# Two recurrence projections taken from the mixer's first block and turned by transposes

## The chip, the cores and the metric

The kernel runs on one core of a Trainium2 chip. The metric is the time of one execution in device microseconds (us). Before the change the median of three runs is 940.21 us (939.73 to 942.36).

## The reference, cut to what matters

The model is an encoder of two layers over 256 tokens of width 1024. Each layer is a half-weighted SwiGLU block, a mixer and a second half-weighted SwiGLU block, each with its own norm; here is the mixer.

```
h = rms_norm(x, mix_norm[l])
proj = h @ w_in[l]                       # 256 x 1792
xr, gate, q, k, v = split(proj, 512 | 512 | 512 | 128 | 128)
y_rec = recurrent_group(xr, gate, ...)   # conv of 4 taps along time, gates, scan in both directions
y_att = windowed_gqa(q, k, v, ...)       # 8 heads, 2 of keys and values
x = x + concat(rms_norm(y_rec), rms_norm(y_att)) @ w_out[l]
```

The change concerns the first 256 of the 512 columns of xr, that is two of its four tiles of 128 channels, and k and v together (256 columns).

## The kernel before, in words

All matrix products are made to near float32 precision from two parts: a value is split into a rounded high part (fp32r) and the rest, and three products are added: high by high, low by high, high by low. So each product of 8 tiles of 128 rows takes 24 matmuls. The engines are named as in the profile: PE is TensorE, DVE is VectorE, ACT is ScalarE, POOL is GpSimd, SP is SyncE.

Weights come in as 1 MB pieces called raw (256 columns of w_in for 1024 rows) by DMAs that SP issues (L248) into three buffers. ACT writes the high part wh (L303; for a few, DVE does, L301) and DVE the low part wl (L304); this happens some units ahead of use (prefetch, prep_one). A raw buffer is loaded anew when the last half made from it is done. Halves lie in a ring of eight slots; the first two halves of the mixer, named kv, lie in two other tiles (EXTRA).

At a boundary between stages (L588 to L620) TensorE finishes the last stage's output, then transposes the normed activations of tokens 0 to 127 (L535), runs head(0), transposes those of tokens 128 to 255, and runs head(1). In the mixer, head(t) (L846) makes keys and values with the tokens as rows: 24 matmuls, each with 256 columns of weights moving (L552). Both token halves lie in one PSUM bank, that ACT copies to kv_t at once (L855). In a SwiGLU stage head(t) (L690) has 24 matmuls of 512 columns (L697), and a bank for each token half.

Then the mixer's body follows the list ORDER (L59), unit by unit. A letter and a digit are one unit: x is one tile of xr, computed with channels as rows (unit, L840: 24 matmuls of 256 columns, L560 to L562, into a bank of its own), after which DVE runs the convolution on it straight out of PSUM in four steps (conv: L877, L879 twice, L880). k turns the keys by two transposes (L864). q is one tile of queries, l the gate matmuls of the recurrence (L900 to L902), L one pair of heads' logits (L965 to L967) with the softmax's first steps on DVE (L974), g the gate, P and V the rest of the attention. Units take their banks in turn from four (bank("gc"): two of ps_g, two of ps_c).

The order on PE, SP and POOL is the order in which the code is written. On ACT and DVE a scheduler sets it when the program is built; on the chip it is fixed, and each engine takes its instructions strictly in that order.

Of the kernel before, what the change touches and what calls it, by code (L numbers as in the profile page):

```python
# [8 lines left out]
F32 = mybir.dt.float32  # L9
F32R = mybir.dt.float32r  # L10
AF = mybir.ActivationFunctionType
# [6 lines left out]
KD = DM // 128  # L18
DFF = 2816
NM = DFF // 128  # L20
T = 256
# [34 lines left out]
CUT = 3  # L56
RCUT = 1
EARLY = 1
ORDER = "x0 k0 x1 q0 l0 q1 l1 L0 x2 L1 x3 g0 l2 P0 q2 l3 V0 P1 s0 L2 g1 c0 c1 q3 V1 P2 L3 c2 y0 g2 y1 V2 P3 g3 c3 V3 D0 y2 y3 r0 O0 r1 O1 r2 r3 R0 R1 R2 R3 S0".split()  # L59
HEAD = 2  # L60
VO = 6
VG = 1
# [5 lines left out]
def encoder_kernel(  # L68
# [31 lines left out]
    pe, act, dve, pool = nc.tensor, nc.scalar, nc.vector, nc.gpsimd  # L100

    def P(name, bufs, **kw):
        return ctx.enter_context(tc.tile_pool(name=name, bufs=bufs, **kw))
# [9 lines left out]
    sum_p = P("sum", 1)  # L113
# [11 lines left out]
    def bank(pool_):  # L125
        if pool_ == "gc":
            turn.append(turn.pop(0))
            pool_ = turn[0]
        return {"a": ps_a, "b": ps_b, "g": ps_g, "c": ps_c}[pool_].tile([128, 512], F32, tag=pool_, name="ps_" + pool_)
# [9 lines left out]
    def add_raw(src, shape):  # L139
        raws.append((src, shape))  # L140
        return len(raws) - 1

    def add_half(name, pieces, form):
        index[name] = len(halves)
        halves.append((name, pieces, form))
        if name[0][1] != 1 or name[1:] not in EXTRA:
            ring.append(name)
            turns[name] = len(ring) - 1

    def cols(w, c):  # L150
        return add_raw(w[:, c:c + 256].rearrange("(k p) c -> p k c", p=128), "kc")

    def rows(w, r):
        return add_raw(w[r:r + 256, :].rearrange("(k p) c -> p k c", p=128), "rc")

    def col_half(name, r, j):
        add_half(name, [(r, j * 128, 0, 128)], "kc")

    def head_half(name, r, j):
        add_half(name, [(r, j)], "kh")  # L160
# [26 lines left out]
        down(NM // 2 - 1)  # L187

    def plan_mix(st, wi, wo):
        r = cols(wi, 1536)  # L190
        for j in range(2):
            head_half((st, "kv", j), r, j)
        chunk = {}

        def chunk_of(n, p):
            if (n, p) not in chunk:
                chunk[n, p] = cols(wi, {"x": 0, "g": 512, "q": 1024}[n] + p * 256)
            return chunk[n, p]

        for n, i in ORDER:  # L200
            i = int(i)
            if n in "xg":
                col_half((st, {"x": "xr", "g": "gt"}[n], i), chunk_of(n, i // 2), i % 2)
            elif n == "q":
                add_half((st, "q", i), [(chunk_of("q", h), i * 64, h * 64, 64) for h in range(2)], "kc")
        for p in range(4):
            r = rows(wo, p * 256)
            for j in range(2):
                add_half((st, "o", 2 * p + j), [(r, j)], "rc")
# [103 lines left out]
    def prefetch(target):  # L313
        while state["half"] <= min(target, state["cap"], len(halves) - 1):
            j = state["half"]
            n = turns.get(halves[j][0], 0)
            if n >= SLOTS and ring[n - SLOTS] not in used:
                return
            with ExitStack() as behind:
                for ins in state["behind"]:  # L320
                    behind.enter_context(tc.issue_after(ins.ins))
                prep_one()

    def W(*name):
        prefetch(index[name] + state["ahead"])
        return slot_t[name]

    def done(name):
        used.add(name)
        del slot_t[name]  # L330

    eye_t = const.tile([128, 128], F32, name="eye_t")
# [159 lines left out]
    cur = {}  # L492
# [52 lines left out]
    def natural(outs, ws, t):  # L545
        ts_ = slice(t * 128, (t + 1) * 128)
        xh, xl = cur["h"], cur["l"]
        for p in range(3):
            for k in range(KD):
                for dst, w in zip(outs, ws):  # L550
                    c = slice((k % 4) * 256, (k % 4) * 256 + 256)
                    pe.matmul(dst, (xh, xh, xl)[p][:, k, ts_], w[k // 4][p % 2][:, c],  # L552
                              start=(p == 0 and k == 0), stop=(p == 2 and k == KD - 1))

    def proj(dst, w, t0, t1):
        wh, wl = w
        xh, xl = cur["h"], cur["l"]
        for k in range(KD):
            ks = slice(k * 128, (k + 1) * 128)
            pe.matmul(dst, wh[:, ks], xh[:, k, t0:t1], start=(k == 0), stop=False)  # L560
            pe.matmul(dst, wh[:, ks], xl[:, k, t0:t1], start=False, stop=False)  # L561
            pe.matmul(dst, wl[:, ks], xh[:, k, t0:t1], start=False, stop=(k == KD - 1))  # L562
# [264 lines left out]

    def mix(l):
        st = (l, 1)
        ps_x = {}  # L830
        xch_t, xcl_t = {}, {}
        xc_t, ge_t, a_t, yh_t, yl_t = {}, {}, {}, {}, {}
        q_t = mix_p.tile([128, NT, T], F32R, tag="q", name="q_t")
# [3 lines left out]
        kv_t = mix_p.tile([128, 2, 256], F32, tag="kv", name="kv_t")  # L837
        late = {}

        def unit(name, i):  # L840
            ps = bank("gc")[:, 0:T]
            proj(ps, W(st, name, i), 0, T)
            done((st, name, i))
            return ps

        def head(t):  # L846
            if t == 0:
                ps_x["kv"] = bank("gc")
            ps = ps_x["kv"]
            natural([ps[:, t * 256:t * 256 + 256]], [[W(st, "kv", j) for j in range(2)]], t)  # L850
            if t == 1:
                for j in range(2):
                    done((st, "kv", j))
                new_tiles()
                act.activation(out=kv_t.rearrange("p t c -> p (t c)"), in_=ps, func=AF.Copy)  # L855

        def new_tiles():
            late["w"] = w_p.tile([128, 2 * NT, T], F32, tag="w", name="w_t")
            late["i"] = mix_p.tile([128, 2 * NT, T], F32, tag="i", name="i_t")
# [6 lines left out]
            dve.tensor_sub(out=kl_t, in0=ps[:, 0:T], in1=k_t.bitcast(F32))  # L866

        def xr(i):
            ps = unit("xr", i)
            with tc.high_priority(offset=MIXF):  # L870
                conv(i, ps)

# [202 lines left out]
        def att_mm(k, t, hfs, fin):  # L1075
            if t not in acc_a:
                acc_a[t] = [bank("ab"[t]) for _ in range(2)]
            stream(acc_a[t], yh_t[4 + k], yl_t[4 + k], W(st, "o", 4 + k), t, hfs, k == 0, k == 3)
            if fin:
                done((st, "o", 4 + k))  # L1080

        def tail(t, part):
            if part in (0, 1):
                for k in range(4):
                    att_mm(k, t, (0,), False)
            if part == 0 and "O1" not in ORDER:
                o_split(1)
# [10 lines left out]
        def body():  # L1098
# [17 lines left out]
            def stats(_):  # L1116
# [5 lines left out]
                    "L": att_logits, "P": att_pt, "V": att_pv, "D": den, "O": o_split, "f": lambda _: turn.reverse()}  # L1122
            for n, i in ORDER:
                step[n](int(i))
                if n == "D":
                    load_gain(3 * l + 2)

        return head, body, tail, evac

    engines = mybir.EngineType  # L1130
    with tc.manual_schedule(engines={engines.PE, engines.SP, engines.Pool}):
# [18 lines left out]
        for s in range(3 * DEPTH):  # L1150
            _, body, tail, evac = stages[s]
            body()
            n = s + 1
# [53 lines left out]
```

## Time and profile before

| | |
|---|---|
| median of 3 runs | 940.21 us |
| profiled execution | 940.3 us |
| its span, first to last instruction | 938.5 us |
| granted TensorE clock, mean | 0.999 of full speed |
| PE busy | 925.9 us, 99% of the span |
| DVE busy | 696.5 us, 74% |
| ACT busy | 544.7 us, 58% |

A row of the timeline has the start of an instruction (or of several alike), its duration, the engine, the line of the kernel, the operation, the tile written and the tiles read, the shape and the count; in square brackets is the engine's idle time before it, and what ended that. Matmuls overlap, so the distance between the starts of two groups tells what a group costs, not its duration. The first layer's mixer runs from about 199.7 to 288 us; the second layer's has the same rows 458.8 us later.

### The profile page before, as it was taken

The numbers are of one execution on the slowest core, as the hardware profiler recorded it, in microseconds if no ns is written. First come the engines' busy times: TensorE is split into PE (matmuls) and PEld (weight loads), VectorE is DVE, ScalarE is ACT, GpSimd is POOL, SyncE is SP. The second block draws the span as 40 slices with busy tenths as digits, with TensorE's granted clock in tenths as the row PEclk, the third lists the DMA queues.
The fourth block names the chain that finished last, engine by engine and source line by source line (L and its number), as shares of the span: only waits on it lengthen the run. The fifth ranks groups of instructions, "written<-read, shape, count | busy, mean of one in ns | idle before, by whom it ended". The sixth has DMA issues, their size and how long they took to land.

```text
span 938.5 us, 13682 instructions
## 1 busy us (share of the span) xinstructions
PE 925.9 (99%) x5288; PEld 804.8 (86%) x5288; DVE 696.5 (74%) x1212; ACT 544.7 (58%) x1006; POOL 37.0 (4%) x58
## 2 busy tenths in 40 slices
PE   8999999999999999999999999999999999999997
PEld 7888888889988888888888888888999888888885
DVE  6877666759998866666688666666799887666663
ACT  7755555547865655555466555554687565555542
POOL 4100000000010000000030000000000100000000
PEclk9999999999999999999999999999999999999999
DMA  8966955614255866565557565655162566665521
GB/s 279 304 211 200 326 192 183 228 64 154 91 157 179 262 197 191 179 192 196 175 174 252 181 186 198 199 179 179 49 223 68 180 233 203 197 196 182 184 86 45
DMA packets 124993, 172.54 MB, mean 184 GB/s; under 512 B 3920, under 2 KB 108792, under 8 KB 124928
## 3 DMA queue, kind: packets, MB, share of 16 engines
q1 hardware_dynamic: 122192, 166.21, 54.7%
q0 software_dynamic: 2288, 4.87, 1.6%
q8 instruction: 41, 0.67, 0.3%
q10 hardware_dynamic: 448, 0.59, 0.2%
q14 instruction: 24, 0.20, 0.1%
HBM read 170.59 MB, written 3.16 MB: 185 GB/s over the span
## 4 chain that ended last, share of the span: by engine, by line
PE 92%; ACT 2%; DVE 2%; DMA 1%; issue 1%; POOL 0%; POOLq 0%; DVEq 0%; ACTq 0%
PE ps_g L572 16%; PE ps_c L572 15%; PE ps_g L571 7%; PE ps_c L571 7%; PE ps_a L581 5%; PE ps_a L583 4%; PE ps_a L582 4%; PE ps_b L582 4%; PE ps_b L583 4%; PE ps_b L581 4%; PE ps_g L697 2%; PE ps_c L697 2%; PE ps_a L1010 1%; PE ps_g L561 1%; PE ps_g L560 1%; PE ps_g L562 1%
## 5 line engine op out<-in xcount | busy, mean ns | idle before, releaser
L304 DVE TENSOR_TENSOR wl<-raw,wh 128x1024 fp32r<-128x1024 f32 (+1 forms) x320 | 367.4, 1157 | 106.3 <-ACT wh L303 101.9
L303 ACT ACTIVATE wh<-raw 128x1024 fp32r<-128x1024 f32 (+1 forms) x306 | 301.6, 1000 | 89.0 <-PE ps_b L583 61.8
L572 PE MATMUL ps_g<-xhl,wh 128*128 128x512 f32 x640 | 231.5, 396 | 1.5 <-DVE hl L746 1.5
L572 PE MATMUL ps_c<-xhl,wh 128*128 128x512 f32 x640 | 231.2, 396 | 0.0
L571 PE MATMUL ps_g<-xhl,wl 128*128 128x256 f32 x560 | 156.5, 279 | 0.0
L571 PE MATMUL ps_c<-xhl,wl 128*128 128x256 f32 x560 | 156.2, 279 | 0.0
L572 PEld LDWEIGHTS ps_g<-xhl,wh 128*128 128x128 f32 x640 | 120.3, 188 | 24.6 <-issue 1.7
L572 PEld LDWEIGHTS ps_c<-xhl,wh 128*128 128x128 f32 x640 | 120.2, 188 | 22.8
L571 PEld LDWEIGHTS ps_g<-xhl,wl 128*128 128x128 f32 x560 | 105.6, 189 | 3.5
L571 PEld LDWEIGHTS ps_c<-xhl,wl 128*128 128x128 f32 x560 | 105.5, 188 | 3.5
L581 PE MATMUL ps_a<-wh,hh 128*128 128x512 f32 x168 | 65.8, 392 | 0.0
L581 PE MATMUL ps_b<-wh,hh 128*128 128x512 f32 x168 | 65.7, 391 | 0.0
L583 PE MATMUL ps_b<-wh,hl 128*128 128x512 f32 x168 | 65.4, 389 | 0.0
L582 PE MATMUL ps_b<-wl,hh 128*128 128x512 f32 x168 | 65.4, 389 | 0.0
L583 PE MATMUL ps_a<-wh,hl 128*128 128x512 f32 x168 | 65.4, 389 | 0.0
L582 PE MATMUL ps_a<-wl,hh 128*128 128x512 f32 x168 | 65.4, 389 | 0.0
L757 ACT ACTIVATE sg<-ps_g 128x256 f32<-128x256 f32 x40 | 15.4, 385 | 63.5 <-PE ps_g L572 63.5
L757 ACT ACTIVATE sg<-ps_c 128x256 f32<-128x256 f32 x40 | 15.3, 383 | 55.3 <-PE ps_c L572 54.6
L758 DVE TENSOR_TENSOR sg<-ps_g,sg 128x256 f32<-128x256 f32 x40 | 17.0, 425 | 32.1 <-ACT sg L757 32.1
L757 ACT ACTIVATE su<-ps_c 128x256 f32<-128x256 f32 x40 | 15.3, 382 | 38.7 <-PE ps_c L572 38.7
L582 PEld LDWEIGHTS ps_a<-wl,hh 128*128 128x128 f32 x168 | 31.6, 188 | 6.9
L583 PEld LDWEIGHTS ps_a<-wh,hl 128*128 128x128 f32 x168 | 31.5, 188 | 6.9
(320 smaller groups left out, 1579.2 us busy)
## 6 DMA issues: line engine op xcount, KB each, us to landing
raw<-in_ffn_w_down_dram SPq DMA_DIRECT2D x44, 1024.0 KB, 5.0
raw<-in_ffn_w_gate_dram SPq DMA_DIRECT2D x43, 1024.0 KB, 5.4
raw<-in_ffn_w_up_dram SPq DMA_DIRECT2D x43, 1024.0 KB, 5.4
raw<-in_w_in_dram SPq DMA_DIRECT2D x14, 1024.0 KB, 5.4
raw<-in_w_out_dram SPq DMA_DIRECT2D x8, 1024.0 KB, 7.3
lb<-ld POOLq DMA_DIRECT2D x1, 2048.0 KB, 14.8
bias_t<-lb POOLq DMA_DIRECT2D x1, 1536.0 KB, 12.5
gain<-in_ffn_norm_dram SPq DMA_DIRECT2D x3, 512.0 KB, 4.3
```

What stands on the lines that cost most here:

```text
L303: act.activation(out=h3, in_=src, func=AF.Copy)
L304: dve.tensor_sub(out=l3, in0=src, in1=h3.bitcast(F32))
L560: pe.matmul(dst, wh[:, ks], xh[:, k, t0:t1], start=(k == 0), stop=False)
L561: pe.matmul(dst, wh[:, ks], xl[:, k, t0:t1], start=False, stop=False)
L571: pe.matmul(dst[:, 0:T], wl[:, ks], x2[:, 0, k, :], start=False, stop=False)
L572: pe.matmul(dst, wh[:, ks], x2[:, :, k, :], start=(k == 0), stop=(k == KD - 1))
L581: pe.matmul(acc[hf], ah[:, ts_], wh[:, cs], start=first, stop=False)
L582: pe.matmul(acc[hf], ah[:, ts_], wl[:, cs], start=False, stop=False)
L583: pe.matmul(acc[hf], al[:, ts_], wh[:, cs], start=False, stop=last)
L697: pe.matmul(ps, x, w[k // 2][p % 2][:, k % 2 * 512:k % 2 * 512 + 512], start=(p == 0 and k == 0), stop=(p == 2 and k == KD - 1))
L757: act.activation(out=s, in_=ps[:, T:2 * T], func=AF.Copy)
L758: dve.tensor_tensor(out=s, in0=ps[:, 0:T], in1=s, op=ALU.add)
```

## The change

Keys and values and the first two tiles of xr are computed together. The head of the mixer now has the form of a SwiGLU head: 24 matmuls per token half, with 512 columns of weights moving (256 of keys and values, 256 of xr), one bank per token half. Four weight halves are made for it (form "gu", each from both raw pieces, 256 columns of each) in place of two of keys and values and two of xr. ACT copies the two parts of each bank apart, to kv_t and to a new tile xn_x. The units x0 and x1 no longer multiply: each turns its tile by two transposes of 128 x 128. x0 and x1 write into the two halves of one bank, where x0 had a bank of its own and x1 another. ORDER puts q0 ahead of x0, and x2 ahead of the first gate unit l0; from x3 on it is the same.

```diff
-ORDER = "x0 k0 x1 q0 l0 q1 l1 L0 x2 L1 x3 g0 l2 P0 q2 l3 V0 ...
+ORDER = "q0 x0 k0 x1 q1 x2 l0 L0 l1 L1 x3 g0 l2 P0 q2 l3 V0 ...
...
     def plan_mix(st, wi, wo):
-        r = cols(wi, 1536)
-        for j in range(2):
-            head_half((st, "kv", j), r, j)
-        chunk = {}
+        chunk = {("x", 0): None}
+        r = cols(wi, 1536), cols(wi, 0)
+        for q in range(4):
+            add_half((st, "kv", q), [(r[0], q, 0), (r[1], q, 1)], "gu")
...
         for n, i in ORDER:
             i = int(i)
+            if n == "x" and i < 2:
+                continue
...
         def head(t):
-            if t == 0:
-                ps_x["kv"] = bank("gc")
-            ps = ps_x["kv"]
-            natural([ps[:, t * 256:t * 256 + 256]], [[W(st, "kv", j) for j in range(2)]], t)
+            ps = bank("gc")
+            ts_ = slice(t * 128, (t + 1) * 128)
+            w = [W(st, "kv", q) for q in range(4)]
+            for p in range(3):
+                for k in range(KD):
+                    x = cur["l" if p == 2 else "h"][:, k, ts_]
+                    pe.matmul(ps, x, w[k // 2][p % 2][:, k % 2 * 512:k % 2 * 512 + 512],
+                              start=(p == 0 and k == 0), stop=(p == 2 and k == KD - 1))
+            act.activation(out=kv_t[:, t, :], in_=ps[:, 0:T], func=AF.Copy)
+            xn_x[t] = sum_p.tile([128, T], F32, tag=("sg", "su")[t], name="xn_x")
+            act.activation(out=xn_x[t], in_=ps[:, T:2 * T], func=AF.Copy)
             if t == 1:
-                for j in range(2):
-                    done((st, "kv", j))
+                for q in range(4):
+                    done((st, "kv", q))
                 new_tiles()
-                act.activation(out=kv_t.rearrange("p t c -> p (t c)"), in_=ps, func=AF.Copy)
...
         def xr(i):
-            ps = unit("xr", i)
+            if i < 2:
+                if i == 0:
+                    ps_x["x"] = bank("gc")
+                ps = ps_x["x"][:, i * T:(i + 1) * T]
+                for t in range(2):
+                    pe.transpose(ps[:, t * 128:(t + 1) * 128], xn_x[t][:, i * 128:(i + 1) * 128], eye_t)
+            else:
+                ps = unit("xr", i)
             with tc.high_priority(offset=MIXF):
                 conv(i, ps)
```

Line numbers in the following lists are those of the file they belong to: the changed one has conv at L892 to L895, k0's transposes at L872 and those of x0 and x1 at L882. A name's number tells buffers apart, and "waits" names the engine whose count an instruction waits for.

On PE before the change, from the end of x0 over the keys' transposes into x1:

```order
L562 MATMUL ps_g<-xhl,wl 128x256
L864 MATMUL ps_c<-eye_t,kv_t 128x128 x2
L560 MATMUL ps_g<-xhl,wh 128x256
L561 MATMUL ps_g<-xhl,wh 128x256
L562 MATMUL ps_g<-xhl,wl 128x256
```

And on PE after it, from the end of q0 over x0, k0 and x1 to the start of q1:

```order
L564 MATMUL ps_c_2200<-xhl_2080,wl_2010 128x256
L882 MATMUL ps_g_2227<-eye_t_111,xn_x_2144 128x128 [waits PE_49]
L882 MATMUL ps_g_2227<-eye_t_111,xn_x_2196 128x128 [waits Activation_49]
L872 MATMUL ps_c_2239<-eye_t_111,kv_t_1973 128x128 [waits PE_49]
L872 MATMUL ps_c_2239<-eye_t_111,kv_t_1973 128x128
L882 MATMUL ps_g_2227<-eye_t_111,xn_x_2144 128x128 [waits DVE_49]
L882 MATMUL ps_g_2227<-eye_t_111,xn_x_2196 128x128
L562 MATMUL ps_g_2255<-xhl_2080,wh_2015 128x256 [waits PE_49]
```

Where x1 multiplied without a wait, it now has two transposes into the bank of x0 (ps_g_2227), the first of which waits for DVE. The count in the program is the one that the last of x0's four conv steps (L895) gives.

On DVE before the change, from x0's conv to the start of x1's:

```order
L877 TENSOR_SCALAR xc_2211<-ps_g_2186,par_117 128x256 [waits PE_49]
L866 TENSOR_TENSOR kl_t_1972<-ps_c_2220,k_t_1971 128x256 [waits Activation_49]
L879 SCALAR_TENSOR_TENSOR xc_2211<-ps_g_2186,par_117,xc_2211 128x254 [waits DVE_49]
L879 SCALAR_TENSOR_TENSOR xc_2211<-ps_g_2186,par_117,xc_2211 128x255 [waits DVE_49]
L880 SCALAR_TENSOR_TENSOR xc_2211<-ps_g_2186,par_117,xc_2211 128x255 [waits DVE_49]
L301 CAST wh_2312<-raw_2157 128x1024 [waits DMAHW3_49]
L877 TENSOR_SCALAR xc_2250<-ps_g_2225,par_117 128x256 [waits PE_49]
```

And on DVE after it, from the low part of the weights of x3 over x0's conv to the start of x1's:

```order
L306 TENSOR_TENSOR wl_2165<-raw_2007,wh_2164 128x1024 [waits Activation_49]
L303 CAST wh_2256<-raw_2168 128x1024 [waits DMAHW3_49]
L892 TENSOR_SCALAR xc_2230<-ps_g_2227,par_117 128x256 [waits PE_49]
L1120 SCALAR_TENSOR_TENSOR ql_t_1970<-ps_c_2200,q_t_1969 128x256 [waits Activation_49]
L894 SCALAR_TENSOR_TENSOR xc_2230<-ps_g_2227,par_117,xc_2230 128x254 [waits DVE_49]
L874 TENSOR_TENSOR kl_t_1972<-ps_c_2239,k_t_1971 128x256 [waits Activation_49]
L894 SCALAR_TENSOR_TENSOR xc_2230<-ps_g_2227,par_117,xc_2230 128x255 [waits DVE_49]
L306 TENSOR_TENSOR wl_2257<-raw_2168,wh_2256 128x1024
L895 SCALAR_TENSOR_TENSOR xc_2230<-ps_g_2227,par_117,xc_2230 128x255 [waits DVE_49]
L306 TENSOR_TENSOR wl_2288<-raw_1981,wh_2287 128x8x64
L904 TENSOR_TENSOR xcl_2236<-xc_2230,xch_2235 128x256 [waits Activation_49]
L892 TENSOR_SCALAR xc_2246<-ps_g_2227,par_117 128x256 [waits PE_49]
```

The queries' low part (L1120), the keys' (L874) and a weight split of 128 x 1024 (L306) now stand between the four steps of x0's conv, and the cast of a raw piece that is still on its way (L303) ahead of them.

## Rows read from the trace of the kernel before

**Rows 1.** The page: busy time of each engine over the span.
```profile
PE 925.9 (99%) x5288; PEld 804.8 (86%) x5288; DVE 696.5 (74%) x1212; ACT 544.7 (58%) x1006; POOL 37.0 (4%) x58
```

**Rows 2.** Waits of PE, whole span: us in total, times, longest.
```profile
PE ps_g L572 <- DVE hl L746: 1.5, 1, 1.5
PE ps_b L535 <- DVE xn L517: 0.9, 2, 0.4
```

**Rows 3.** Timeline of PE, the mixer's head, first layer.
```profile
199.72 0.64 PE L552 MATMUL ps_c<-w_w,xhl 128*128 128x256 f32 x4
...
203.13 1.54 PE L535 MATMUL ps_b<-eye_t,xn 128*128 128x128 f32 x8 [0.44 <-DVE xn L517]
...
207.64 0.28 PE L560 MATMUL ps_g<-xhl,wh 128*128 128x256 f32 x1
```

**Rows 4.** Timeline of PE, the next SwiGLU stage's head: its start and its follower.
```profile
288.21 1.98 PE L697 MATMUL ps_c<-wh,xhl 128*128 128x512 f32 x8
...
300.31 0.39 PE L572 MATMUL ps_c<-xhl,wh 128*128 128x512 f32 x1
```

**Rows 5.** Timeline of PE: starts of k0 and q0.
```profile
210.52 0.38 PE L864 MATMUL ps_c<-eye_t,kv_t 128*128 128x128 f32 x2
...
213.61 0.28 PE L560 MATMUL ps_c<-xhl,wh 128*128 128x256 f32 x1
```

**Rows 6.** Timeline of ACT: between SwiGLU's two heads.
```profile
293.86 0.39 ACT L737 ACTIVATE th<-ps_c 128x256 f32<-128x256 f32 x1 [2.77 <-PE ps_c L697]
```

**Rows 7.** Timeline of DVE: conv of x0 and of x1 with what stands between.
```profile
210.72 0.54 DVE L877 TENSOR_SCALAR xc<-ps_g,par 128x256 f32<-128x256 f32 x1 [2.95 <-PE ps_g L562]
...
212.72 0.48 DVE L880 SCALAR_TENSOR_TENSOR xc<-ps_g,par,xc 128x255 f32<-128x255 f32 x1
213.12 0.68 DVE L301 CAST wh<-raw 128x1024 fp32r<-128x1024 f32 x1
213.82 0.54 DVE L877 TENSOR_SCALAR xc<-ps_g,par 128x256 f32<-128x256 f32 x1
214.28 0.42 DVE L889 TENSOR_TENSOR xcl<-xc,xch 128x256 fp32r<-128x256 f32 x1
214.61 0.48 DVE L879 SCALAR_TENSOR_TENSOR xc<-ps_g,par,xc 128x254 f32<-128x254 f32 x1
215.00 1.22 DVE L304 TENSOR_TENSOR wl<-raw,wh 128x1024 fp32r<-128x1024 f32 x1
216.13 0.48 DVE L879 SCALAR_TENSOR_TENSOR xc<-ps_g,par,xc 128x255 f32<-128x255 f32 x1
...
217.12 0.48 DVE L880 SCALAR_TENSOR_TENSOR xc<-ps_g,par,xc 128x255 f32<-128x255 f32 x1
```

**Rows 8.** Timelines: the last conv step of x2 (DVE) and g0's start (PE).
```profile
230.10 0.48 DVE L880 SCALAR_TENSOR_TENSOR xc<-ps_c,par,xc 128x255 f32<-128x255 f32 x1
...
230.63 0.39 PE L560 MATMUL ps_c<-xhl,wh 128*128 128x256 f32 x1
```

**Rows 9.** Raw loads (L248) from 160 to 240 us: issue to landing.
```profile
DMA to landing us min/median/max: 4.9/5.3/8.2
```

**Rows 10.** Timeline of DVE: first and last read of the first logits.
```profile
223.36 0.48 DVE L974 CUSTOM_DVE_ANT_0 pr<-ps_c,bias_t,sink_t 128x256 f32<-128x256 f32 x1 [0.23 <-PE ps_c L967]
...
226.00 0.48 DVE L974 CUSTOM_DVE_ANT_0 pr<-ps_g,bias_t,sink_t 128x256 f32<-128x256 f32 x1
```

**Rows 11.** Timeline of PE: start of q2.
```profile
235.84 0.36 PE L560 MATMUL ps_g<-xhl,wh 128*128 128x256 f32 x1
```

**Rows 12.** ACT, 150 to 262 us, grouped by shape: busy us, mean ns, idle before.
```profile
L303 ACT ACTIVATE wh<-raw 128x1024 fp32r<-128x1024 f32 x18 | 19.0, 1053 | 2.9 <-PE ps_b L583 2.9
...
L303 ACT ACTIVATE wh<-raw 128x512 fp32r<-128x512 f32 x8 | 4.7, 621 | 3.6 <-DMA raw<-in_w_in_dram 3.6
```

**Rows 13.** A PE gap near the start, and the stretch's busy times, clock, DMA.
```profile
10.00:14.00 4.00, 2.76 (x20) 2.08 (x18) 2.88 (x9) 3.60 (x10) 1.63 (x3) 1.00 1.09 353
...
13.46 1.16 PE L424 MATMUL ps_b<-eye_t,xn 128*128 128x128 f32 x8 [1.14 <-DVE xn L414]
```

More of the change, by code (lines that the diff above doesn't have):

```diff
@@ L58 @@
 EARLY = 1
-ORDER = "x0 k0 x1 q0 l0 q1 l1 L0 x2 L1 x3 g0 l2 P0 q2 l3 V0 P1 s0 L2 g1 c0 c1 q3 V1 P2 L3 c2 y0 g2 y1 V2 P3 g3 c3 V3 D0 y2 y3 r0 O0 r1 O1 r2 r3 R0 R1 R2 R3 S0".split()
+ORDER = "q0 x0 k0 x1 q1 x2 l0 L0 l1 L1 x3 g0 l2 P0 q2 l3 V0 P1 s0 L2 g1 c0 c1 q3 V1 P2 L3 c2 y0 g2 y1 V2 P3 g3 c3 V3 D0 y2 y3 r0 O0 r1 O1 r2 r3 R0 R1 R2 R3 S0".split()
 HEAD = 2
@@ L829, in mix @@
         st = (l, 1)
-        ps_x = {}
+        ps_x, xn_x = {}, {}
         xch_t, xcl_t = {}, {}
```

## The prediction

> **What bounds the kernel now.** I read the page's busy times first. TensorE is busy for 925.9 of 938.5 us, VectorE for 74% and ScalarE for 58% [rows 1]: TensorE is the bound, and only what it executes or waits for can move the end. Then I read its waits over the whole span. The mixer's share is small: 0.9 us in two waits, one in each layer, for the normed activations of the second token half [rows 2]. From the mixer's head on, the timeline shows one matmul after another. So a microsecond taken from TensorE's list is a microsecond gained, provided that what is left does not wait. In such a kernel a change loses by making TensorE wait, and that is what I look for, with the order of the instructions beside the durations of the trace.
>
> **The change part by part.** All times are of one layer; the second layer has the same rows. Its edits are the wide head, the turned tiles, the new order with the shared bank, and the weight halves.
>
> *The wide head.* Before, the head runs from 199.72 to 207.64, 7.92 us, including the second token half's transposes and a wait of 0.44 [rows 3]. x0 follows up to k0's start, 207.64 to 210.52, 2.88 us for 24 matmuls or 0.12 each [rows 3, 5]. k0 and x1 take 210.52 to 213.61, 3.09, which is 0.21 for k0's two transposes and x1's 2.88 [rows 5]. Together 7.92 + 2.88 + 3.09 = 13.89. After, the head has the form of the SwiGLU head, which takes 288.21 to 300.31, 12.10 us, with its own transposes and handover [rows 4]. There, one ScalarE operation of 0.39 stands between the two token halves [rows 6]; here two copies of the same width do, ahead of the casts that the second half's matmuls read. The SwiGLU row shows no separate price for such an operation, so I bound it by nothing and by 0.39, and take 0.15, since most of it lies beside the transposes. Then come three pairs of transposes (x0, k0, x1) at 0.21. Sum: 12.10 + 0.15 + 0.63 = 12.88, against 13.89: **-1.0** (from -1.3, with the copies hidden and the turned tiles partly beside other work, to 0). q0 only changes places: its 24 matmuls remain.
>
> *The shared bank.* This costs more than the head gives. In the order after, x1's first transpose waits for VectorE, for the last of x0's four conv steps. Before, x1 had a bank of its own and no wait, and 2.88 us of matmuls between x0 and the next reader. Now only k0's 0.21 us stand between. An existing wait of this kind shows its price: x2's last conv step starts at 230.10, takes 0.48, and g0, which takes that bank, starts at 230.63, 0.05 later [rows 8].
>
> When does x0's conv end? Counting from the head's start at 199.72: 12.25 for the head and 2.88 for q0 place x0's transposes at 214.85; they end some 0.42 later (0.38 is the recorded duration of a pair [rows 5], 0.04 the handover), so VectorE can start at 215.27, when TensorE reaches x1 too (214.85 + 0.42). Alone, with one small operation between, x0's conv took 210.72 to 213.20, 2.48 us [rows 7]. In the order after, three operations stand between its steps: two low parts of 128 x 256 and a weight split of 128 x 1024. From the distances in x1's old conv [rows 7] the steps cost 0.46 (213.82 to 214.28), 0.33 for a low part (to 214.61), 0.39 (to 215.00), another 0.33, 0.39 again, 1.13 for the split (215.00 to 216.13), and 0.48 for the last: 3.51. With 0.05 TensorE goes on at about 218.85: a wait of **+3.6**. The nearest row that includes a split is x1's old conv, 213.82 to 217.60, 3.78 [rows 7], so I stay near it. The low end is 2.48 less k0's 0.21, about 2.3. The high end: ahead of the conv, VectorE has the cast of a raw piece whose load waits for the low part of x3's weights. I place that low part behind the second half's transposes (about 207.0), ScalarE's 1.05 [rows 12] and VectorE's 1.22 [rows 7]: 209.3, an estimate. Loads land 4.9 to 8.2 us after issue, median 5.3 [rows 9]; with the cast's 0.68 [rows 7] VectorE is free at 214.9, 215.3 or 218.2. The median is just in time, the worst adds 2.9, so the high end is 6.5.
>
> The rows of before show no engine reading one half of a bank while another writes the other half; the order says that this program waits. The Trainium skill, page "PSUM — Partial Sum Buffer", section "PSUM bank collisions raise a hardware error", says why it is right to: two engines must be kept apart by bank and group of 32 partitions, and disjoint columns do not help. Were waits set by columns alone, the time would be that of the second rival below; by this page's rule it is the forecast's. No run here shows a collision.
>
> *What is queued behind.* VectorE is now late when the units behind need it. x1's conv, with its splits, is covered by q1 and x2 (5.76). Then x2 stands directly ahead of l0. L0's second bank waits for x2's conv: it needs some 2.1 (2.48 less a low part of 0.33), and TensorE covers it with l0's 12 matmuls (1.44) and L0's first products (0.2): +0.5. L1's second bank waits for the softmax's reads of L0. Before, VectorE took from 223.36 to 226.48 for all of those, with two other operations between them [rows 10], and x2's 2.88 stood in front of L1. Now only l1's 1.44 do: the reads end some 3.0 behind L0, L1's second bank is due at 1.64: +1.4. x3's bank waits for a gate's copy by ScalarE, with little to cover it; I take 0.2. Against this, g0's old handover goes, -0.2 by estimate. Sum **+1.9**; bounds 0 (VectorE catches up, since it waits nowhere else in this stretch) and 2.5 (every reader late by one more operation). From x3 on the order is the same and the lateness is simply carried: before, TensorE had no wait there.
>
> *Weights.* Of eight raw halves, four splits of 1024 become eight of 512 columns: 2 x 0.62 against 1.05 on ScalarE [rows 12], some 0.8 us in all. ScalarE has idle time in that stretch (3.6 us for a DMA ahead of the 512s alone [rows 12]), which hides it; without that cover the head would start that much later. SP and POOL issue the same list in the same order; one raw piece is issued later because its buffer is freed only by the fourth wide half. I cost it at nothing and bound it at +1.0.
>
> **Sum.** -1.0 + 3.6 + 1.9 = +4.5 in each layer, +9.0 for two. The profiled execution took 940.3 us (span 938.5 and 1.8 around it): 949.3. It stood 0.1 above the median of 940.21, so the forecast is **949.2**.
>
> **Rivals.**
> - *Only the first wait.* VectorE is late at x1, but x1, x2 and the first logits catch up behind it; -1.0 + 3.6 = +2.6, twice is +5.2: 945.4. For it: VectorE is busy 74% and idles elsewhere. Against it: l1 covers half of what x2 covered before.
> - *No wait at x1 (not slower).* x1's transposes go on beside x0's conv, or the conv is done before they are reached. Then -1.0 twice remains: 938.2. For it: the two halves of the bank share no column. Against it: the wait stands in the order, and the conv would have to end within k0's 0.21, where its steps alone take 2.48 [rows 7]. It decides from the point where that conv is shorter than what TensorE has in between. In a milder form the train costs as much as the head gives, and the time is the same.
> - *The clock falls.* The idle stretch at x1 of 3.6 us drops the granted clock, and q1's 24 matmuls behind it run at the lower level, 1.2 instead of 2.4 GHz: another 2.88 per layer, 5.8 in all: 955.0. The longest idle gap near here, 1.14 us at 13.46, shows a granted clock of 1.00 around it [rows 13], which speaks against it; but it is a third as long. The Trainium skill, page "TensorE: Matmul & The Clock Gate", Part 1, says that an idle TensorE is put back to half rate; rows 13 do not show it for a short gap, and no gap of 3.6 us is in the trace.
> - *The load is late.* The cast ahead of x0's conv waits for a load of 8.2 instead of 5.3 us: +2.9 per layer, again about 955.0. Rows 9 have such a load, as the extreme.
>
> **How the numbers follow.** The forecast gets 0.63, the first wait alone 0.15, no wait 0.10 (0.04 faster, 0.06 the same with the head's gain lost to small waits), the clock 0.05, the late load 0.07. A measurement of this kernel tells about 0.3%, 2.8 us, from no change. Faster is 0.04, same 0.06, slower 0.90: the others all lie at +5.2 or more. The range goes down from 949.2 by the train's and the wait's low ends in part, through the first rival's 945.4 to 942.5, and up to 955.5, through the late load and the clock. Left out are the not slower rival's 0.10 and some 0.08 for extremes.
>
> **What would show it.** Right: between k0's and x1's transposes TensorE idles about 3.6 us, released by VectorE's last conv step on x0; then waits of about half a microsecond and over a microsecond on VectorE at the second banks of L0 and L1; the head from its first matmul to q0's takes 12.1 to 12.3; q2, at 235.84 before [rows 11], starts at about 240.3; the granted clock stays 1.00. VectorE's idle time ahead of the cast shows whether the load was late. Wrong: no idle at x1 (then the bank is not shared in the way that counts), or a head near 13, or idle time in front of the head's first matmul, which would mean that the wide weight halves are late. A time under 943 would say that VectorE catches up; over 955 that the load or the clock joins in.

## The result, and the profile after

The changed kernel takes 955.36 us (median of 4 runs, 953.0 to 955.88), the kernel before 940.22. The ratio estimated from the runs is 1.0154, with a 95% interval of 1.0141 to 1.0168 (the two medians alone give 1.016). The ratios below are estimated in the same way, each against the kernel before as it was timed beside that run (medians of 939.8 to 940.2). The changed kernel is slower, as forecast, but by 15 us where 9 were forecast: the time lies at the upper end of the range.

The page of the changed kernel, busy times:

```profile
PE 932.4 (98%) x5200; PEld 806.4 (85%) x5200; DVE 697.6 (73%) x1220; ACT 546.5 (57%) x1020; POOL 37.0 (4%) x58
```

TensorE has 88 instructions fewer than in [rows 1] and is busy for 6.5 us longer. It multiplies about as many columns as before (in each layer 48 matmuls of 512 columns stand for 96 of 256, and four transposes are new), so more work is not the reason; a lower clock would be one. Its waits over the span come next (total, times, longest):

```profile
PE ps_g L882 <- DVE xc L895: 7.0, 2, 3.5
PE ps_c L980 <- DVE stm L989: 1.6, 2, 0.8
...
PE ps_c L982 <- DVE ql_t L1120: 0.8, 2, 0.4
PE ps_c L562 <- DVE ge L947: 0.5, 2, 0.3
PE ps_c L980 <- DVE xc L895: 0.4, 2, 0.2
```

The one mixer wait of [rows 2], L535 for the normed activations, is gone. In its place stands x1's wait (L882) for the last step of x0's conv, with waits at the logits (L980, L982) and, once in each layer, at a gate unit (L562) behind it. The timeline of TensorE, first layer, gives their places:

```profile
199.57 0.63 PE L855 MATMUL ps_c<-w_w,xhl 128*128 128x512 f32 x2
...
212.00 0.28 PE L562 MATMUL ps_c<-xhl,wh 128*128 128x256 f32 x1
...
214.88 0.38 PE L882 MATMUL ps_g<-eye_t,xn_x 128*128 128x128 f32 x2
215.09 0.38 PE L872 MATMUL ps_c<-eye_t,kv_t 128*128 128x128 f32 x2
218.97 0.69 PE L882 MATMUL ps_g<-eye_t,xn_x 128*128 128x128 f32 x2 [3.50 <-DVE xc L895]
219.31 0.56 PE L562 MATMUL ps_g<-xhl,wh 128*128 128x256 f32 x1
...
223.50 0.28 PE L562 MATMUL ps_c<-xhl,wh 128*128 128x256 f32 x1
...
232.70 0.38 PE L980 MATMUL ps_c<-k_t,q_t 64*128 64x256 f32 x1 [0.81 <-DVE stm L989]
...
233.83 0.38 PE L562 MATMUL ps_g<-xhl,wh 128*128 128x256 f32 x1 [0.16 <-ACT i_t L924]
...
241.91 0.36 PE L562 MATMUL ps_g<-xhl,wh 128*128 128x256 f32 x1
```

Read the starts, not the durations. The head takes 212.00 - 199.57 = 12.43 us; q0 stands to 214.88. At 218.97 x1 has waited 3.50. Then q1, 24 matmuls, takes 219.31 to 223.50, 4.19 us, where 24 such matmuls took 2.88 before [rows 3, 5]. The windows with the granted clock (the third number from the end) say why:

```profile
216.00:219.00 3.00, 0.03 (x1) 0.03 (x1) 3.00 (x7) 2.28 (x5) 0.00 (x0) 0.95 0.00 0
219.00:222.00 3.00, 3.00 (x14) 3.00 (x15) 3.00 (x6) 0.37 (x1) 0.00 (x0) 0.50 0.00 0
222.00:226.00 4.00, 4.00 (x35) 4.00 (x34) 3.17 (x7) 0.69 (x2) 0.00 (x0) 0.98 0.55 166
```

TensorE idles in the first stretch, runs at 0.50 of full speed, 1.2 GHz, in the second, and is back in the third. The Trainium skill, page "TensorE: Matmul & The Clock Gate", Part 1, says that an idle TensorE falls to half rate; here the trace agrees, 0.50 behind an idle stretch of 3.50 us. In the second layer the wait at x1 is 3.52 us. There TensorE begins again at full speed, at 684.82, and the clock falls some 1.5 us later; q1 takes 4.21 us. The clock falls once more behind the second pair's logits:

```profile
700.00:702.00 2.00, 2.00 (x11) 2.00 (x11) 1.67 (x10) 2.00 (x8) 0.00 (x0) 0.50 0.00 0
702.00:704.00 2.00, 2.00 (x13) 2.00 (x13) 0.69 (x1) 2.00 (x7) 0.00 (x0) 0.65 0.00 0
```

What holds TensorE is on VectorE's timeline, whose old rows are [rows 7]:

```profile
208.08 1.23 DVE L306 TENSOR_TENSOR wl<-raw,wh 128x1024 fp32r<-128x1024 f32 x1
214.80 0.69 DVE L303 CAST wh<-raw 128x1024 fp32r<-128x1024 f32 x1 [5.49 <-DMA raw<-in_w_in_dram]
215.41 0.54 DVE L892 TENSOR_SCALAR xc<-ps_g,par 128x256 f32<-128x256 f32 x1
...
218.44 0.47 DVE L895 SCALAR_TENSOR_TENSOR xc<-ps_g,par,xc 128x255 f32<-128x255 f32 x1
...
226.58 0.54 DVE L892 TENSOR_SCALAR xc<-ps_c,par 128x256 f32<-128x256 f32 x1 [1.40 <-PE ps_c L564]
```

It stands idle for 5.49 us ahead of the cast, whose load has not landed, and begins x0's conv at 215.41. Before, it began at 210.72 [rows 7]. From there it works without a pause until 225.2, through the convs of x0 and x1. Then it has caught up: ahead of x2's conv, at 226.58, it is VectorE that waits, 1.40 us, for TensorE's matmuls of x2. So the late conv holds TensorE at x1, but not at L0 and L1 behind it. There VectorE does its part as soon as its inputs are ready, and TensorE comes too early: l0's 12 matmuls stand between x2 and L0, and l1's 12 between L0 and L1, where x2's 24 stood before.

### The profile page after: what moved, and what is told of

Same layout as the page of the kernel before. It is cut to its first block, busy times and chain, and to the rows that moved or that the text cites. A ratio compares the mean times of both kernels' runs of the same rounds, so it can differ in the third digit from the quotient of the medians.

```text
span 954.1 us, 13528 instructions
## 1 busy us (share of the span) xinstructions
PE 932.4 (98%) x5200; PEld 806.4 (85%) x5200; DVE 697.6 (73%) x1220; ACT 546.5 (57%) x1020; POOL 37.0 (4%) x58
## 4 chain that ended last, share of the span: by engine, by line
PE 89%; DVE 4%; ACT 3%; DMA 3%; issue 1%; POOL 0%; POOLq 0%; DVEq 0%; ACTq 0%
PE ps_g L574 15%; PE ps_c L574 15%; PE ps_g L573 7%; PE ps_c L573 7%; PE ps_a L583 4%; PE ps_a L585 4%; PE ps_b L585 4%; PE ps_b L583 4%; PE ps_b L584 4%; PE ps_a L584 4%; PE ps_g L699 2%; PE ps_c L699 2%; PE ps_c L855 1%; DMA raw<-in_w_in_dram 1%; PE ps_a L1025 1%
## 5 line engine op out<-in xcount | busy, mean ns | idle before, releaser
L306 DVE TENSOR_TENSOR wl<-raw,wh 128x1024 fp32r<-128x1024 f32 (+1 forms) x324 | 368.1, 1144 | 108.9 <-ACT wh L305 104.3
```

The lines of the kernel that those rows point to most:

```text
L306: dve.tensor_sub(out=l3, in0=src, in1=h3.bitcast(F32))
```

## The experiments

Two theories were set against each other. The *bank theory* takes the prediction's first cost alone: the shared bank makes the wait, and without it the wait and the slow stretch behind it are gone. The *VectorE theory*: VectorE begins its share of the mixer some 4.7 us later and cannot make it up, so the wait is only the first place where that shows. A third question was the clock. A third cause, the closer spacing of the units that the new order brings, stands in the prediction (its +1.9) but in neither theory; the runs below show it.

**A bank each.** The shared bank is undone:

```diff
-                if i == 0:
-                    ps_x["x"] = bank("gc")
-                ps = ps_x["x"][:, i * T:(i + 1) * T]
+                ps = bank("gc")[:, 0:T]
```

> x0 and x1 get a bank each; all else as in the changed kernel. Bank theory: the wait of 3.5 us ahead of x1 and the half-speed stretch of TensorE behind it (q1 took 4.2 instead of 2.9 us) are the loss; both go, 4.8 us per layer, 9.6 in all: about 945.8 us. VectorE theory: VectorE is behind by its own work from x0's conv on (some 9.7 us without a pause), so the wait moves to the first gate units and logits, whose banks wait for the convs of x1 and x2; TensorE's clock may stay, and only 2 us per layer come back: about 951.5 us.

Measured: 953.87 us, ratio 1.0145 (1.0129 to 1.0160). TensorE's waits in the first layer, and one window:

```profile
216.19 0.39 PE L562 MATMUL ps_c<-xhl,wh 128*128 128x256 f32 x1 [0.58 <-DVE ql_t L1118]
223.55 0.35 PE L913 MATMUL ps_g<-xch,gh_t 128*128 128x256 f32 x1 [0.62 <-DVE xc L893]
225.86 0.38 PE L978 MATMUL ps_g<-k_t,q_t 64*128 64x256 f32 x1 [0.82 <-ACT i_t L922]
228.54 0.58 PE L913 MATMUL ps_g<-xch,gh_t 128*128 128x256 f32 x1 [0.79 <-DVE xc L893]
```

```profile
229.00:235.00 6.00, 6.00 (x30) 5.55 (x30) 4.69 (x19) 5.68 (x17) 0.00 (x0) 0.50 0.65 255
```

The wait of 3.50 us is gone and 1.5 us of time with it, which is within the two intervals, and not the 9.6 of the bank theory. The wait came back in four pieces, three of them released by VectorE, at q1 and the gates (L913), and one by ScalarE, at the logits (L978). In the first layer the clock fell there instead.

**All transposes at once.** The same bank, but x1's transposes stand in x0, ahead of the conv:

```diff
+                    for j in range(2):
+                        for t in range(2):
+                            pe.transpose(ps_x["x"][:, j * T + t * 128:j * T + (t + 1) * 128], xn_x[t][:, j * 128:(j + 1) * 128], eye_t)
```

> All four transposes of x0 and x1 stand in x0, in the shared bank, ahead of x0's conv; x1 is only its conv. No transpose waits for a conv. Bank theory: 4.8 us per layer come back, about 945.8 us. VectorE theory: l0 now takes the shared bank and waits for x1's conv instead (some 2 us), L0's second bank for x2's conv; about 1.7 us per layer come back, 952.0 us.

Measured: 954.63 us, 1.0154 (1.0137 to 1.0171): nothing gained, against the bank theory. The VectorE theory's 952.0 is missed too, and l0 does not wait for x1's conv. The new waits are L0 for a gate's function on ScalarE (1.09) and l1 for x2's conv (1.44, in the second layer 2.12). The edit also changed VectorE's order: a weight split and the queries' low part now stand ahead of x0's conv, which starts at 217.22, 1.8 us later than in the changed kernel.

**x1 behind q1.** The order becomes q0 x0 k0 q1 x1 x2 l0:

> The order puts q1 ahead of x1, with the shared bank kept: q1's 2.9 us of matmuls cover most of the wait. Bank theory: the idle stretch at x1 shrinks from 3.5 to about 0.6 us, the granted clock stays at 1.00, and 4.2 us per layer come back: about 947.0 us. VectorE theory: x1's conv starts and ends when it did, l0 waits for it, and about 1.7 us per layer come back: 952.0 us.

Measured: 952.73 us, 1.0136 (1.0121 to 1.0151). The idle time at x1 is 0.56 us, as both expected, and the time is near the VectorE theory's (952.0). But l0 does not wait for x1's conv, as that theory had it: waits of 1.39 at L0, for a gate's function on ScalarE, and 1.32 at L1, for the softmax's reads, took its place, and the clock fell behind both.

**Work in the wait.** 26 matmuls of 256 columns go ahead of x1's transposes:

```diff
+                if i == 1:
+                    idle = bank("b")[:, 0:T]
+                    for m in range(26):
+                        pe.matmul(idle, gh_t[:, 0, 0, 0, :], cur["h"][:, m % KD, 0:T], start=(m == 0), stop=(m == 25))
```

> 26 matmuls of 256 columns, whose result nobody reads, stand ahead of x1's transposes (26 x 0.12 = 3.1 us inside a wait of 3.5 us). Clock theory: TensorE has work in the wait, so the granted clock stays at 1.00, q1 takes 2.9 instead of 4.2 us, and although 52 matmuls are added in all the kernel becomes faster by 1.3 us per layer: about 952.7 us; the second layer's other slow stretch (x3, 1.5 us) may go too, 951.2. Rival, that the slow stretch is only covered waiting for VectorE: no change, 955.4 us.

Measured: 953.86 us, 1.0144 (1.0128 to 1.0159). q1 takes 2.94 us (219.07 to 222.01) instead of 4.19, so the slow stretch at x1 was the clock's and came from the idle time. But the clock fell at L1 instead, behind waits of 0.37 and 0.87, and x3 took 4.29. So a further run filled those as well, with 3 and 7 more:

```diff
+                    if i == 1 and b == 0:
+                        idle, f = bank("b")[:, 0:T], (3, 7)[e]
+                        for m in range(f):
+                            pe.matmul(idle, gh_t[:, 0, 0, 0, :], cur["h"][:, m % KD, 0:T], start=(m == 0), stop=(m == f - 1))
```

> As the kernel that fills x1's wait with 26 matmuls whose result nobody reads, and 3 and 7 more of them ahead of the first and second bank of the second pair's logits, where the clock fell in that run (0.37 and 0.87 us of waiting). Clock theory: the granted clock stays at 1.00 through the first half of the mixer, x3 takes 3.0 instead of 4.3 us, and 1.3 us per layer come back against 953.9: about 951.2 us. Rival, that TensorE is held by VectorE and ScalarE at the units behind anyway: the clock stays, but the time with it at 953.9, with longer waits at the third logits.

Measured: 952.63 us, 1.0132 (1.0115 to 1.0149). The windows of this run:

```profile
216.00:219.00 3.00, 2.71 (x24) 2.51 (x22) 3.00 (x7) 2.40 (x5) 0.00 (x0) 1.00 0.00 0
219.00:222.00 3.00, 3.00 (x27) 3.00 (x26) 3.00 (x6) 0.15 (x1) 0.00 (x0) 1.00 0.00 0
...
233.00:236.00 3.00, 3.00 (x27) 3.00 (x27) 2.60 (x12) 3.00 (x11) 0.00 (x0) 1.00 0.01 4
```

With 72 matmuls more, the clock stays at 1.00 through the whole stretch, x3 takes 2.98 us, and the kernel is 2.7 us faster than the changed one by the medians; the two intervals against before overlap a little, so this is likely rather than certain. That is what the lower clock costs on balance, with the added matmuls paid. The changed kernel's own runs point the same way: the one with the highest mean clock, 0.996, is the shortest (953.0 us), the one with the lowest, 0.992, the longest (955.88). The other 12.5 us are not the clock's: x1's last conv step still starts at 222.85, 0.5 us sooner than in the changed kernel.

**The order by itself.** The kernel before, with the new order only (x0 k0 x1 q0 l0 q1 l1 L0 x2 L1 becomes q0 x0 k0 x1 q1 x2 l0 L0 l1 L1):

> The kernel before, with its own head and a bank for each unit, but with the changed order of units (q0 ahead of x0, x2 ahead of l0). VectorE theory: x0's conv starts 2.9 us later with nothing else changed, VectorE cannot make that up, and TensorE waits at the first logits, some 1.9 us per layer and 0.8 later at the third logits: about 945.5 us. Rival, that only the wide head with its shared bank costs: no change, 940.2 us.

Measured: 945.57 us, 1.0061 (1.0047 to 1.0075), the VectorE theory's number. Its reason does not show in the trace. VectorE's, TensorE's and ScalarE's rows:

```profile
212.79 0.70 DVE L301 CAST wh<-raw 128x1024 fp32r<-128x1024 f32 x1 [1.69 <-DMA raw<-in_w_in_dram]
213.40 0.54 DVE L877 TENSOR_SCALAR xc<-ps_c,par 128x256 f32<-128x256 f32 x1
```

```profile
225.31 0.38 PE L965 MATMUL ps_c<-k_t,q_t 64*128 64x256 f32 x1 [1.36 <-ACT i_t L909]
```

```profile
222.71 0.47 ACT L908 ACTIVATE w_t<-ps_g,hba 128x256 f32<-128x256 f32 x1 [0.45 <-PE ps_g L902]
```

x0's conv starts 2.7 us later than before, but no unit from x1 to l0 waits for VectorE. TensorE waits at L0, 1.36 us, for one of l0's gate functions, and ScalarE began these functions as soon as the first of l0's two banks was done (222.71). What the new order took away is the cover: before, q1 and l1 stood between l0 and L0, now nothing does. From the head's start to q2's the first layer takes 38.57 us, 2.45 more than before [rows 3, 11], with +1.75 at L0 and +0.86 at L1, at full clock. In the second layer the clock fell as well, behind the same wait of 1.36 us, and the whole mixer takes 4.7 us more there:

```profile
690.00:692.00 2.00, 2.00 (x13) 1.78 (x14) 1.94 (x7) 2.00 (x8) 0.00 (x0) 0.50 0.39 152
```

The third logits, where the theory expected 0.8 us, do not wait. So the new order costs some 2.5 us per layer at full clock, with no shared bank and no wide head, and by its spacing; that the theory's sum met the time was luck. The order makes two moves (q0 ahead of x0, x2 ahead of l0), and no run has one without the other. **The old order in the changed kernel** is the counterpart:

> The changed kernel with the order of before (x0 first, q0 behind x1, x2 behind the first logits). VectorE theory: x0's conv can start at the head's end, 212.4 instead of 215.4, but the cast of the raw piece that lands at 214.8 stands between its steps, so the conv ends only some 2 us earlier than in the changed kernel (about 216.4); x1's transposes wait 3.9 us, what follows is some 2 us less late: about 951.5 us. Bank theory: the wait grows from 3.5 to 3.9 us and the slow stretch stays: about 956 us.

Measured: 950.61 us, 1.0114 (1.0099 to 1.0130), near the VectorE theory's number again. The wait at x1 is 2.83 us (both theories had 3.9), x0's transposes now wait 0.64 for ScalarE's copy of the new tile, and at L0 and L1 no wait is left. So the two parts of the change nearly add up: the order alone costs 5.5 us (945.57 against 940.09), the rest without it 10.5 (950.61 against 940.09), and both together 15.1.

**Early convs.** All four transposes right behind the head (x0 x1 k0 q0 q1 l0 l1 L0 x2 L1), and ScalarE in VectorE's place for the cast that waited for its load (VG = 0):

> Directly behind the head all four transposes of x0 and x1 together, then k0, q0, q1, l0, l1, L0, x2, L1; and ScalarE casts the raw piece that VectorE cast. VectorE theory: it starts on x0's conv at 212.4, 3 us sooner than in the changed kernel; the low part of that raw piece still holds it from about 214.6 to 217, x1's conv ends near 220, and l0 waits 1.5 us for it; 3 to 4 us per layer come back: about 948 us. Bank theory: no transposes wait, so 4.8 us per layer come back, 945.8 us.

Measured: 945.95 us, 1.0062 (1.0048 to 1.0076). VectorE begins at 213.50 and x1's last conv step at 219.54; 9.4 us of the 15 come back. The number is the bank theory's (945.8). But the run takes back the new order as well (l1 stands between l0 and L0 and x2 between L0 and L1) and moves a cast, so it shows the remedy and does not tell the causes apart.

**GpSimd for four low parts.** The same, with the low parts of gate 0 and 1 and queries 2 and 3 taken from VectorE:

```diff
+            if name[0][1] == 1 and name[1:] in (("gt", 0), ("gt", 1), ("q", 2), ("q", 3)):
+                pool.tensor_tensor(out=l3, in0=src, in1=h3.bitcast(F32), op=ALU.subtract)
```

> As the kernel with the early convs, and GpSimd instead of VectorE makes the low parts of four weight halves (gate 0 and 1, queries 2 and 3) that stood between the convs: 4.7 us of VectorE's work per layer go. VectorE theory: both convs are done by 218, before q1's matmuls end, TensorE waits nowhere, and the head's gain of 1.0 us per layer is left: about 938.2 us. If GpSimd takes over 3 us for a half, the raw pieces are freed late and part of that is lost: up to 944 us. Bank theory: no better than without GpSimd, 946 to 948 us.

Measured: 943.94 us, 1.0040 (1.0027 to 1.0052), the best of the series and still slower than before. The expected 938.2 was missed: 0.64 us of waiting for the new tile's copy, 0.73 for a gate's function on ScalarE ahead of x2 and 0.25 at the third logits are left in each layer, 1.6 of the 2.9 us that each layer missed by (the rest was not traced), and x1's conv ends no sooner than without GpSimd, for a reason told below. In the changed kernel as it stands, the same edit fails altogether:

> The changed kernel, its order and its shared bank kept; only the low parts of four weight halves (gate 0 and 1, queries 2 and 3) go from VectorE to GpSimd, 4.7 us of VectorE's work per layer between the convs. VectorE theory: x0's conv ends 1.1 us sooner (a wait of 2.4 instead of 3.5 us at x1), x1's conv some 3 us sooner, the waits at the logits shrink, but GpSimd's work slows VectorE's reads while it runs; 2 to 3 us per layer come back: about 950.5 us. Bank theory: only the 1.1 us at x1 come back, about 953.2 us.

Measured: 968.87 us, 1.0299 (1.0283 to 1.0315). The wait at x1 shrinks to 2.38, as expected, but ScalarE and TensorE show this:

```profile
227.89 2.00 ACT L305 ACTIVATE wh<-raw 128x1024 fp32r<-128x1024 f32 x2 [4.97 <-DMA raw<-in_w_in_dram]
```

```profile
232.38 0.58 PE L983 MATMUL ps_c<-k_t,q_t 64*128 64x256 f32 x1 [5.01 <-ACT i_t L927]
```

GpSimd's six operations took 10.05 us. ScalarE waits 4.97 us for a load, and the gates' functions stand behind that cast in its order. The load itself was hardly late: it was issued at 222.72, in the changed kernel at 222.49. There ScalarE makes its next cast at 230.53, behind the first gates' functions (from 227.30). So this wait comes from the place that the scheduler gave the cast, and not from a late load. Neither theory had this.

**Spread units.** With k0 x0 x1 q0 q1 l0 l1 x2 L0 x3 L1, and VectorE copying the second half of the new tile; first with GpSimd's low parts, then without:

> The early convs with GpSimd's low parts, and the order k0 x0 x1 q0 q1 l0 l1 x2 L0 x3 L1: two units of projections stand between gates and logits, so that ScalarE's gate functions and VectorE's reads each have 3 us of matmuls beside them; VectorE copies the second token half of the new tile. VectorE theory: what is left of the waits (0.6 us for the copy, 0.2 at l0, 0.7 for a gate's copy) falls to some 0.6 us per layer: about 940 us, at best 939, the kernel before or slightly better. If the gates' functions on ScalarE bind instead: about 943 us.

> The same without GpSimd: VectorE makes all low parts. VectorE theory: its 4.7 us more stand between the convs, l0 waits about 1 us for x1's conv and the logits for x2's conv: about 943 us. If VectorE's work no longer binds in this order: as with GpSimd, 940 us.

Measured: 951.97 us, 1.0121 (1.0108 to 1.0135), and 947.32, 1.0073 (1.0060 to 1.0086). Both missed. In the first, g0 waits 1.83 us for the softmax's reads, the third logits 1.01 and the next gate unit 0.52; without GpSimd the first of these is 0.37 and the others are the same (1.02 and 0.51). Why GpSimd helps with the early convs and harms here was not settled. No version beat the kernel before.

The start of x1's last conv step on VectorE in the first layer, for all kernels:

| kernel | x1's last conv step starts | time, us |
|---|---|---|
| before | 217.12 | 940.2 |
| spread units | 219.26 | 947.3 |
| early convs, GpSimd's low parts | 219.47 | 943.9 |
| early convs | 219.54 | 946.0 |
| spread units, GpSimd's low parts | 219.63 | 952.0 |
| changed, old order | 219.81 | 950.6 |
| before, new order | 221.33 | 945.6 |
| changed, GpSimd's low parts | 221.39 | 968.9 |
| changed, all waits filled | 222.85 | 952.6 |
| a bank each | 222.93 | 953.9 |
| changed, x1's wait filled | 222.97 | 953.9 |
| changed | 223.34 | 955.4 |
| x1 behind q1 | 223.56 | 952.7 |
| all transposes at once | 224.01 | 954.6 |

The time goes with it only loosely: the kernel before with the new order is 5 us faster than the changed one with the old order, although its step starts 1.5 us later. How late VectorE is does not settle the time by itself.

## Why the prediction was right or wrong

The direction, the first wait with its place and size, and the cost behind it were right. The sum was too small by the clock, and by a wait farther on that it put at nothing. First layer, from the head's start to q2's: 36.12 us before [rows 3, 11], 42.34 after, +6.2 where +4.5 was forecast.

- *The wide head, -1.0.* Head 12.43, x0's pair 0.21, k0's 0.21, x1's 0.34: 13.19 against 13.89, so -0.7. The head itself cost 12.43 against the 12.25 taken, with a wait of 0.15 for ScalarE in it; x1's pair ran at the lower clock.
- *The wait at x1, +3.6.* Measured 3.50 of idle time and 0.17 more for the end of k0's pair (218.97 - 215.09 = 3.88, less the 0.21 of the term above): 3.67. VectorE's steps are as listed. The load was just in time, as placed: the cast ran at 214.80. This term was the best. It does not say, and no one should read from it, that a second bank would save the wait: given a bank each, TensorE pays at q1, the gates and the logits, since VectorE is busy without a pause until about 224.
- *What is queued behind, +1.9.* From q1's end to q2 the units differ by x2 -0.18, l0 +0.09, L0 +0.59, l1 +0.09, L1 +1.65, x3 -0.20, g0 -0.10: together +1.94. L0 (+0.5), L1 (+1.4) and the end of g0's old handover were right nearly to the number, and so was their reason, too few matmuls between a unit and the reader of its bank. The term's opening words, that VectorE is late there, were wrong: it had caught up at x2's conv.
- *The clock, a rival at 0.05.* This step failed. The argument from [rows 13], a short gap with full clock, did not carry to one three times as long. q1 cost +1.31 in the first layer and +1.33 in the second, not the 2.88 of the rival, since the clock came back within it or just behind it; in the second layer x2 (3.11 us) and x3 (4.47) lost some 1.7 more. Filling the waits gave back 2.7 us net.
- *"From x3 on the order is the same and the lateness is simply carried."* This failed too. In both layers the third logits and the gate unit behind them take 0.85 us longer (258.49 to 260.65, before 252.43 to 253.74), released by VectorE. VectorE is no later than TensorE there: where its operations are still the same as before it is 5.99 us behind the old times, and TensorE 6.06. But its own order has changed: a scan (L937) now stands ahead of the low part of the queries (L1120) for which the logits wait, where before the scan (L922) came behind it (L1105). The order in the list ORDER is the same from x3 on; the scheduler's order on VectorE is not.

```profile
252.36 0.42 DVE L1105 SCALAR_TENSOR_TENSOR ql_t<-ps_g,q_t 128x256 fp32r<-128x256 f32 x1
252.70 0.68 DVE L922 TENSOR_TENSOR_SCAN i_t<-a_t,i_t 128x256 f32<-128x256 f32 x1
```

```profile
258.02 0.68 DVE L937 TENSOR_TENSOR_SCAN i_t<-a_t,i_t 128x256 f32<-128x256 f32 x1
258.62 0.40 DVE L945 SCALAR_TENSOR_TENSOR x<-x,ps_c 128x256 f32<-128x256 f32 x1
258.93 0.42 DVE L1120 SCALAR_TENSOR_TENSOR ql_t<-ps_g,q_t 128x256 fp32r<-128x256 f32 x1
```

The sum as measured: -0.7 + 3.67 + 1.94 + 1.31 = 6.2, and with 0.85 it is 7.1 in the first layer. The second adds the 1.7 of its own slow stretches, 8.7; together 15.8, less 0.15 by which the first head starts sooner, 15.6, the difference of the two spans. The range held only by its upper end, which the clock and the late load had set. That the clock's rival names 955.0 is luck: it has 5.8 us for the clock, where q1 and the second layer's slow stretches took 4.3, and the third logits 1.7. Of the rivals, only the first wait (945.4) and no wait (938.2) are out. The late load was not needed.

So the runs show several causes. The new order costs some 5 us by its spacing, shown in the kernel before. The wide head with x1's transposes behind x0's conv costs some 10 without that order, and a bank of its own for x1, tried in the new order, gave back 1.5. Of the whole, the lower clock costs some 2.7 us on balance. How much of the rest is VectorE's late start and how much the matmuls that used to run beside the convs was not measured apart.

## What to carry to other kernels

An engine at 74% over the span can be full in the stage that matters: before, VectorE was busy 9.05 of the 10 us from 210 to 220, just where the change puts its work later. Ask of a change two things apart: what it makes the bound engine wait for (x0's conv, with 0.2 us of cover left), and which units it takes from between a bank's writer and its next reader (q1 and l1 ahead of L0). Try the wait's removal on paper: if the same engine is the next releaser, one more bank does not help. When a run meets a theory's number, look who released the waits before believing the theory: the new order alone took 945.57 us where 945.5 were expected, for another reason. And when the bound engine will idle for some microseconds, give a lower clock behind it a real chance.

## What the runs showed of the hardware that was not expected

TensorE's clock fell to 0.50 behind one idle stretch of 3.50 us, and also where several short waits stood close together (0.62, 0.82 and 0.79 us within 5 us, in the kernel with a bank each). One and the same wait need not always do it: in the kernel before with the new order, 1.36 us at L0 left the clock at 1.00 in the first layer and was followed by 0.50 in the second. With the waits filled by matmuls nobody reads, it stayed at 1.00. So useless work was cheaper here than waiting.

While GpSimd made low parts, some of VectorE's operations of the same kind took several times as long. In the run with early convs and GpSimd (GpSimd's row, then VectorE's):

```profile
215.62 11.05 POOL L307 TENSOR_TENSOR wl<-raw,wh 128x1024 fp32r<-128x1024 f32 x6 [13.39 <-ACT wh L305]
```

```profile
216.40 1.92 DVE L909 TENSOR_TENSOR xcl<-xc,xch 128x256 fp32r<-128x256 f32 x1
```

Without GpSimd that operation took 0.42 us; the convs, which read one input from PSUM, kept their 0.48. The Trainium skill, page "SBUF — State Buffer", section "Who interferes with whom", says that a VectorE instruction with two inputs in SBUF contends with a GpSimd instruction that reads SBUF, that one with at most one input in SBUF, outside the two-port modes, does not, and that the shared ports are an exclusive lock: whoever is first blocks the other for its whole length. The trace agrees: 1.92 us instead of 0.42 with two inputs in SBUF, 0.48 as before with one, and the slow operation, begun at 216.40, ends at 218.32, just behind the first of GpSimd's (215.62 to 218.04). GpSimd's six operations, four halves in all, took 11.05 us where VectorE's of these shapes, two of 1.22 and four of 0.68, take 5.2.
